# An eight-core two-layer trunk: weight loads held behind the last residual load, the last tile in halves, and norm sums rounded once to bf16

## The chip, the cores and the metric

The kernel runs on all eight cores of one Trainium2 chip, one batch element per core; the cores do not exchange data. Cores 0 to 3 form one die, cores 4 to 7 the other. The metric is the device time of the slowest core, in microseconds (us). The engines are TensorE (PE in the profile), VectorE (DVE), ScalarE (ACT), GpSimd (POOL) and SyncE (SP, which here only issues transfers).

In the fast state every core was granted about 0.99 of the full TensorE clock. In the slow state the cores of one die, or of both, had a visibly lower clock, and the run took up to 3340 us.

## The reference

It is a decoder trunk for batch 8, sequence 4096 and width 1024. Cut to what matters:

```python
for layer in range(2):
    sh1, sc1, g1, sh2, sc2, g2 = ada_modulation(c, ada_w[layer], ada_b[layer])
    h = rmsnorm(x, norm_mix_g[layer]) * (1.0 + sc1) + sh1
    y = mixer_0(h) if layer == 0 else mixer_1(h)     # projections in, mixing, one projection out
    x = x + g1 * y
    h = rmsnorm(x, norm_ffn_g[layer]) * (1.0 + sc2) + sh2
    hid = jnp.square(jax.nn.relu(h @ w_ff1[layer]))  # 1024 -> 4096
    x = x + g2 * (hid @ w_ff2[layer])                # 4096 -> 1024
return rmsnorm(x, final_g)
```

## The kernel before

Each core works through four stages (mixer 0, feed-forward 0, mixer 1, feed-forward 1), each in eight tiles of 512 positions. Between stages the residual stream `xs` lives in HBM: a stage loads it (`load_x`), norms it, and at its end adds to it piece by piece (`residual`). The program is a graph. A list scheduler, with its own model of costs, fixes one static order per engine, by `key`, and semaphore waits are then put where the graph has a dependency.

The norm sums eight squares in float32. It then splits the sum into two bf16 numbers, so that TensorE can sum over partitions with little loss, which takes two products:

```python
def norm_stats(get, Bn, dst, b_dst, key, adds):
    for c in range(8):                    # squares on ScalarE, adds on GpSimd or VectorE into dst (f32)
        # ... cut ...
    act(... activation(out=sqt[:, 0, :], in_=dst, func=AF.Copy) ...)                        # bf16 part
    dve(... tensor_tensor(out=sqt[:, 1, :], in0=dst, in1=sqt[:, 0, :], op=ALU.subtract) ...) # the rest
    pe([(lambda e, i=i: e.matmul(bk(Bn), onesD, sqt[:, i, :], start=i == 0, stop=i == 1), ...)
        for i in range(2)], [Bn], key)
    # ... cut: Ln, Exp
```

The residual add, and the load of a weight:

```python
def residual(ph, ti, c, B, l, grp, key, after=()):
    s = npiece[0] % 8                                             # eight pieces in turn
    dma("sp", ... e.dma_start(out=piece[:, s, :], in_=ap[:, 0, :]) ..., key - 12, ..., after)   # load
    dve(... scalar_tensor_tensor(out=piece[:, s, :], in0=bk(B), ..., in1=piece[:, s, :], ...), key)  # add
    dma("sp", ... e.dma_start(out=xs_d[ph][ti, :, c, :], in_=piece[:, s, :]) ..., key)          # store

def load_weight(k, name, kind, src, key, after=()):
    # ... cut
    dma("pool", lambda e: e.dma_start(out=v, in_=src), [], [b], key, wsem[k], 2 * 1024 * 1024, after)
```

`after` keeps the scheduler from placing an operation before the other has been placed, and nothing more. The waits on the chip come from `pdeps`, which `after` never enters:

```python
# schedule()
for op in self.ops:
    for d in op.after:
        op.npend += 1
        d.succ.append((op, None))      # an order in the list schedule
# emit_orders()
for pi, pd in enumerate(op.pdeps):     # only these become semaphore waits
    ...
```

In a feed-forward, tile 0 runs its second product in blocks, so that it can begin before all weights are there:

```python
w1 = [load_weight(..., base - 40 + i, after[i:i + 1]) for i in range(8)]
w2 = [load_weight(..., base - 30 + i) for i in range(8)]
for ti in range(ntiles):
    # ... cut: 32 groups of 8 products of 128x512 (w1), relu, square
    if ti + 1 < ntiles:
        stage_a(ph, ti + 1, hT, hb, b + TF - 60, b + TF - 45, "dve", [begun])   # load, norm, modulate
    # ... cut: 256 products (w2), then residual adds, or in the last stage the final norm and the stores
```

## Time and profile before

Before the change the kernel took 2825.24 us, the median of three runs (2820.91 to 2830.31).

The opening lines of the page of the kernel before: span, then each engine's busy time, share of the span and instructions.

```profile
span 2822.9 us, 41582 instructions; the slowest of 8 cores (2789.6 to 2822.9 us)
...
PE 2721.0 (96%) x14197; PEld 1267.0 (45%) x14197; DVE 1266.1 (45%) x2171; ACT 1246.0 (44%) x1974; POOL 521.7 (18%) x697
```

TensorE is what bounds the kernel. Inside a stage, time is its number of products; what else there is to win lies at the joints between stages. The cores also differ by 33 us, although all run the same program on data of the same shapes.

I cut the span at landmarks of TensorE: the first value projection of mixer 0, the last output projection of each mixer, the first product with `w_ff2` in each feed-forward, the first value projection of mixer 1, the last main product. For the slowest core (7) and as means over the eight cores of the same execution:

| stage (us) | core 7 | mean |
|---|---|---|
| start | 68.2 | 68.2 |
| mixer 0 | 580.2 | 578.9 |
| joint 0: last projection to first `w_ff2` product | 47.5 | 45.0 |
| feed-forward 0 | 844.6 | 846.0 |
| mixer 1 | 359.9 | 359.5 |
| joint 1 | 69.7 | 57.2 |
| feed-forward 1 | 836.4 | 836.3 |
| tail: last main product to the end | 16.4 | 16.4 |

Three cores (0, 5 and 6) waited nowhere of note at joint 1, and took 46.8 to 46.9 us; the slowest took 69.7.

The list of waits of TensorE on core 7 before, 540 to 760 us and then 1820 to 2000 us. A line names the waiting engine and source line, what it waited for, the total in us, the number of waits and the longest.

```profile
PE ps L713 <- DVE sb_arena L704: 5.6, 2, 3.8
PE ps L665 <- ACT sb_arena L662: 1.3, 1, 1.3
...
PE ps L713 <- DVE sb_arena L704: 17.3, 4, 6.3
```

L704 is the residual add. TensorE's first feed-forward products (L713) wait for a bank of PSUM, which comes free when the add has read it. L665 is the norm product. The add itself waits for its load. This is the view of that one line, 1830 to 1940 us, with what it waited for, us and times:

```profile
  DMA sb_arena<-xs: 36.4, 4
```

What is in the way of those loads are weights. The timeline of GpSimd on core 7 before, at the end of mixer 1; columns are start, length, engine, line, operation, and in brackets the idle time before and its releaser:

```profile
1856.00 0.59 POOL L570 DMA_DIRECT2D sb_arena<-w_ff  x1 [10.83 <-PE ps L1146]
...
1877.41 1.15 POOL L1193 TENSOR_TENSOR sb_arena<-sb_arena 128x512 bf16<-128x512 f32 x1 [5.34 <-DVE sb_arena L1188]
```

Weights of the next stage go out as soon as the buffer that they overwrite is read (L1146 is the value projection), before the last tile's multiplies (L1193).

The tail on core 7 before, from the timeline: last residual add, square, add, the subtract of the split (L663), eight multiplies, stores (the steps between are left out).

```profile
2806.95 0.75 DVE L1057 SCALAR_TENSOR_TENSOR sb_arena<-ps,sb_arena 128x512 f32<-128x512 f32 x1 [4.64 <-PE ps L1032]
...
2810.05 0.69 DVE L663 TENSOR_TENSOR sb_arena<-sb_arena 128x512 bf16<-128x512 f32 x1 [0.83 <-ACT sb_arena L662]
...
2813.08 5.39 DVE L1065 SCALAR_TENSOR_TENSOR sb_arena<-sb_arena 128x512 f32<-128x512 f32 x8 [2.34 <-ACT sb_arena L669]
2813.91 4.97 SPq L1069 DMA_DIRECT2D out<-sb_arena  x8
```

### The profile page before, as it was taken

The page shows a single profiled execution, that of the slowest core. Times are in us where ns is not written, and L with a number is a line of the kernel's source. Part 1 is how long each engine was busy: PE and PEld are TensorE (multiplying, and loading weights), DVE is VectorE, ACT ScalarE, POOL GpSimd, SP SyncE. Part 2 cuts the span into 40 slices and gives each one's busy share as a digit, 9 for nine tenths or more (in the row PEclk, how much of TensorE's full clock was granted, in tenths as well). Part 3 has the DMA queues.
Part 4 walks back from the last instruction along what each step waited for, and adds up shares of the span by engine and source line. Part 5 has one row for each costly group of instructions (what it writes and reads, how often), then busy time and mean ns, then how long its engine had stood idle before and what let it go on. Part 6 is the DMA issues. An engine that isn't in the chain of part 4 may idle for free.

```text
span 2822.9 us, 41582 instructions; the slowest of 8 cores (2789.6 to 2822.9 us)
## 1 busy us (share of the span) xinstructions
PE 2721.0 (96%) x14197; PEld 1267.0 (45%) x14197; DVE 1266.1 (45%) x2171; ACT 1246.0 (44%) x1974; POOL 521.7 (18%) x697
## 2 busy tenths in 40 slices
PE   3999999999999999999999999997999999999997
PEld 1444444444444444444444444443444444444443
DVE  3567777771332232231323777752343243342332
ACT  5788888862333132141224765642343243242330
POOL 5456555440000000000002444230000000000000
PEclk9999999999999999999999999998999999999999
DMA  9743344479423323223354465576021020220110
GB/s 190 146 120 106 105 105 106 116 141 186 140 53 79 81 65 91 68 64 104 78 109 136 137 185 155 168 140 158 31 90 60 31 90 16 75 90 1 60 60 30
DMA packets 111375, 279.96 MB, mean 99 GB/s; under 512 B 12352, under 2 KB 12864, under 8 KB 104384
## 3 DMA queue, kind: packets, MB, share of 16 engines
q1 hardware_dynamic: 92016, 198.65, 22.4%
q0 software_dynamic: 19152, 78.65, 16.7%
q8 instruction: 117, 1.92, 0.3%
q14 instruction: 90, 0.74, 0.1%
HBM read 284.59 MB, written 67.11 MB: 125 GB/s over the span
## 4 chain that ended last, share of the span: by engine, by line
PE 81%; DMA 8%; ACT 4%; issue 3%; DVE 2%; POOL 2%; another core or an unknown queue 0%; SPq 0%; DVEq 0%; ACTq 0%; POOLq 0%
PE ps L713 38%; PE ps L1032 31%; DMA xs<-sb_arena 4%; PE ps L1146 3%; PE ps L1200 3%; PE ps L981 2%; PE ps L954 2%; DMA sb_arena<-xs 2%; DMA sb_arena<-w_in 1%; ACT L408 1%; DMA sb_arena<-x 1%; PE ps L665 1%; PE ps L610 0%; ACT sb_arena L691 0%; PE ps L1183 0%
## 5 line engine op out<-in xcount | busy, mean ns | idle before, releaser
L713 PE MATMUL ps<-sb_arena 128*128 128x512 bf16 x6144 | 1376.7, 381 | 29.4 <-DVE sb_arena L704 22.9
L713 PEld LDWEIGHTS ps<-sb_arena 128*128 128x128 bf16 x6144 | 595.5, 98 | 733.3 <-issue 46.7
L1032 PE MATMUL ps<-sb_arena 128*128 128x512 bf16 x4096 | 890.3, 379 | 0.0
L1021 ACT ACTIVATE sb_arena<-ps 128x512 bf16<-128x512 f32 x512 | 305.0, 597 | 874.3 <-PE ps L713 806.8
L1032 PEld LDWEIGHTS ps<-sb_arena 128*128 128x128 bf16 x4096 | 398.8, 98 | 477.4
L1023 DVE TENSOR_TENSOR sb_arena<-sb_arena 128x512 bf16<-128x512 bf16 x512 | 218.5, 427 | 482.7 <-ACT sb_arena L1021 480.1
L658 ACT ACTIVATE sb_arena<-sb_arena 128x512 f32<-128x512 f32 x280 | 172.9, 625 | 383.3 <-DVE sb_arena L1057 333.5
L704 DVE SCALAR_TENSOR_TENSOR sb_arena<-ps,sb_arena 128x512 f32<-128x512 f32 x192 | 142.9, 746 | 435.6 <-PE ps L1032 312.9
L687 DVE SCALAR_TENSOR_TENSOR sb_arena<-sb_arena 128x512 f32<-128x512 f32 x256 | 195.1, 788 | 42.5 <-ACT sb_arena L669 23.1
L691 ACT ACTIVATE sb_arena<-sb_arena 128x512 bf16<-128x512 f32 x256 | 179.0, 721 | 66.0 <-DVE sb_arena L687 51.0
L408 ACT ACT_TABLE_LOAD x138 | 177.1, 1283 | 39.6 <-PE ps L713 23.5
L629 POOL DMA_DIRECT2D sb_arena<-ada_w x72 | 39.5, 549 | 807.1 <-PE ps L610 785.5
L660 POOL TENSOR_TENSOR sb_arena<-sb_arena 128x512 f32<-128x512 f32 x112 | 149.4, 1334 | 181.2 <-ACT sb_arena L658 171.7
L1057 DVE SCALAR_TENSOR_TENSOR sb_arena<-ps,sb_arena 128x512 f32<-128x512 f32 x64 | 48.0, 751 | 268.1 <-PE ps L1032 267.4
L660 DVE TENSOR_TENSOR sb_arena<-sb_arena 128x512 f32<-128x512 f32 x168 | 116.0, 690 | 83.2 <-ACT sb_arena L658 75.5
L981 PE MATMUL ps<-sb_arena 128*128 128x512 bf16 x512 | 119.8, 379 | 0.0
L1146 PE MATMUL ps<-sb_arena 128*128 128x512 bf16 x512 | 119.5, 379 | 0.0
L1200 PE MATMUL ps<-sb_arena 128*128 128x512 bf16 x512 | 117.8, 379 | 0.3 <-POOL sb_arena L1193 0.2
L1193 POOL TENSOR_TENSOR sb_arena<-sb_arena 128x512 bf16<-128x512 f32 x64 | 75.3, 1193 | 70.1 <-DVE sb_arena L1188 68.6
L1200 PEld LDWEIGHTS ps<-sb_arena 128*128 128x128 bf16 x512 | 50.0, 98 | 61.0 <-issue 1.2
L981 PEld LDWEIGHTS ps<-sb_arena 128*128 128x128 bf16 x512 | 49.5, 98 | 57.7 <-issue 0.2
L1146 PEld LDWEIGHTS ps<-sb_arena 128*128 128x128 bf16 x512 | 49.2, 98 | 55.3
(113 smaller groups left out, 1713.1 us busy)
## 6 DMA issues: line engine op xcount, KB each, us to landing
xs<-sb_arena SPq DMA_DIRECT2D x192, 256.0 KB, 3.7
sb_arena<-xs SPq DMA_DIRECT2D x96, 512.0 KB, 6.2
sb_arena<-xs SPq DMA_DIRECT2D x192, 256.0 KB, 4.1
sb_arena<-w_ff POOLq DMA_DIRECT2D x32, 1024.0 KB, 16.2
sb_arena<-ada_w POOLq DMA_DIRECT2D x72, 256.0 KB, 4.0
sb_arena<-x SPq DMA_DIRECT2D x64, 256.0 KB, 3.6
out<-sb_arena SPq DMA_DIRECT2D x64, 256.0 KB, 3.3
sb_arena<-x SPq DMA_DIRECT2D x24, 512.0 KB, 5.9
```

What stands on the lines that cost most here:

```text
L408: eng.preload_act_table_set(op.table)
L658: act(lambda e, c=c, ap=ap: e.activation(out=tmp[:, c % 2, :], in_=ap, func=AF.Square), [b], [tmpb[c % 2]], key, c_act(512))
L660: G.add(adds, lambda e, c=c: e.tensor_tensor(out=dst, in0=dst, in1=tmp[:, c % 2, :], op=ALU.add), [b_dst, tmpb[c % 2]], [b_dst], key, c_po ...
L687: dve(lambda e, c=c: e.scalar_tensor_tensor(out=tmp[:, c % 2, :], in0=xT[:, c, :], scalar=s1c[:, q, c:c + 1], in1=inv, op0=ALU.mult, op1=A ...
L691: act(lambda e, c=c: e.activation(out=hT[:, c, :], in_=tmp[:, c % 2, :], func=AF.Identity, bias=mod(l, g, c), scale=1.0), [tmpb[c % 2], mo ...
L713: parts = [(lambda e, kc=kc: e.matmul(bk(B), w[:, kc, col0:col0 + 128], hT[:, kc, :], start=kc == 0, stop=kc == 7), [wb, hb[kc]], c_mm(512 ...
L981: pe([(lambda e, kk=kk, c=c, B=B, wv=wv, yc=yc: e.matmul(bk(B), wv[:, kk, (c % 4) * 128:(c % 4) * 128 + 128], yc[:, kk, :], start=kk == 0, ...
L1021: act(lambda e, B=B, q=q: e.activation(out=rt[:, q, :], in_=bk(B), func=AF.Relu), [B], [rtb[q]], k, c_act(512, True))
L1023: dve(lambda e, q=q, fc=fc: e.tensor_tensor(out=hid[:, fc, :], in0=rt[:, q, :], in1=rt[:, q, :], op=ALU.mult), [rtb[q]], [hidb[fc]], k, c_ ...
L1032: return pe([(lambda e, fc=fc, c=c, B=B: e.matmul(bk(B), w2[fc // 4][0][:, fc % 4, c * 128:(c + 1) * 128], hid[:, fc, :], start=fc == 0, s ...
L1146: o = pe([(lambda e, kc=kc, g=g, hh=hh, B=B, hT=hT: e.matmul(bk(B), hT[:, kc, g * 128:(g + 1) * 128], win[2 + hh][0][:, kc, :], start=kc == 0,
L1200: pe([(lambda e, kk=kk, c=c, B=B, wv=wv: e.matmul(bk(B), wv[:, kk, (c % 4) * 128:(c % 4) * 128 + 128], ymix[:, kk, :], start=kk == 0, stop ...
```

## The change

It has three parts. (1) The norm's sum is written as bf16 by the last add, so that one product replaces two and the copy and the subtract go. (2) The last tile of the last stage is computed in halves of 256 positions, so that the norm, the multiplies and the stores of the first half run under the products of the second, and what follows the last product is half as wide. (3) Weight loads are "held" behind the last residual load of the stage before, and in mixer 0 the projections of the tile before the last get earlier keys.

```diff
@@ norm_stats: part 1
-                G.add(adds, lambda e, c=c: e.tensor_tensor(out=dst, in0=dst, in1=tmp[:, c % 2, :], op=ALU.add), ...
-            act(lambda e: e.activation(out=sqt[:, 0, :], in_=dst, func=AF.Copy), ...
-            dve(lambda e: e.tensor_tensor(out=sqt[:, 1, :], in0=dst, in1=sqt[:, 0, :], op=ALU.subtract), ...
-            pe([(lambda e, i=i: e.matmul(bk(Bn), onesD, sqt[:, i, :], ...) for i in range(2)], [Bn], key)
+                to, b_to = (dst, b_dst) if c < 7 else (sqt[:, 0, :], sqb[0])
+                G.add(adds, lambda e, c=c, to=to: e.tensor_tensor(out=to, in0=dst, in1=tmp[:, c % 2, :], op=ALU.add), ...
+            pe([(lambda e: e.matmul(bk(Bn), onesD, sqt[:, 0, :], start=True, stop=True), ...)], [Bn], key)
@@ phase_m0: part 3, layer 0 (ld is the residual's load)
-                    k = b + T0 + (8 + 2 * c if ti + 1 == ntiles else 18 + 4 * c)
+                    k = b + T0 + (18 + 4 * c if ti + 2 < ntiles else 12 + 1.8 * c if ti + 2 == ntiles else 8 + 2 * c)
-                    residual(0, ti, c, B, 0, 2, k, [first])
+                    ld = residual(0, ti, c, B, 0, 2, k, [first])
+            return [()] * 2 + [[ld]] * 14
@@ phase_m1: part 3, layer 1
-            return marks
+            return [[m] for m in marks[:6]] + [[ld]] * 10
@@ phase_ffn
-            w1 = [load_weight(..., base - 40 + i, after[i:i + 1]) for i in range(8)]
-            w2 = [load_weight(..., base - 30 + i) for i in range(8)]
+            w1 = [load_weight(..., base - 40 + i, after[i]) for i in range(8)]
+            w2 = [load_weight(..., base - 30 + i, after[8 + i]) for i in range(8)]
+            def last_tile(ti, b):                                   # part 2
+                for h in range(2):
+                    for c in range(8):
+                        # ... cut: 32 products of 256 columns, residual add, square, add (the 8th square goes
+                        #     to TensorE by itself), for c in (2, 3) a multiply by the gain on GpSimd
+                    # ... cut: norm by two products, Ln, Exp
+                    for c in range(8):
+                        # ... cut: c in (2, 3) multiplied on GpSimd, the six others on VectorE; stores in pairs
+                if final and ti + 1 == ntiles:
+                    last_tile(ti, b)
+                    continue
```

## The prediction

> **What bounds the kernel now.** TensorE is busy 96% of the span (page, first part) and all 760 us from 2000 to 2760 (stretches by engine). 128x512 matmuls start 0.216 us apart (64 in 13.84 us in the chain). The Trainium skill, "TensorE: Matmul & The Clock Gate", section "Wait — 56ns, not 53.3ns?", gives 215.7 ns warm: the trace agrees. Inside a stage only fewer matmuls help; at the joints waits do. On the slowest core (7) these are:
> - start: 33.6 us on adaLN weights, untouched;
> - layer 0 mixer to feed-forward: 5.6 us of TensorE waiting for the residual add;
> - layer 1 mixer to feed-forward: 17.3 us of the same wait (waits list, 1820 to 2000), then clock 0.83 and 0.66 in 1900 to 1940: together about 22 us;
> - end: 16.1 us after the last main matmul (timeline: add 0.75, square 0.63, add 0.69, copy 0.63, subtract 0.69, two matmuls, Ln 0.69, Exp 0.63, eight multiplies 5.39, 4.4 to the end).
> The third is bandwidth: the adds wait 36.4 us for residual loads, whose buffers wait for stores that take over 20 us under weight loads. It falls on cores 1, 3, 4, 7; cores 0, 2, 5, 6, one of each pair, lose at most 1.3 us there and end at 2790 to 2798. The skill's "HBM Reference", "Specifications (TRN2)", says the two cores of a domain share bandwidth; the trace fits, without proving it.
>
> **What the change does.**
> 1. Norm sums: 40 norms lose one matmul, one copy, one subtract. On TensorE 38 x 0.216 = 8 us (estimate from the pitch); the rest is off the path. Expected: -8.
> 2. Last tile in halves: 512 matmuls of 256 columns replace 256 of 512. At 128 columns the trace shows four in 0.39 us, about 55 ns apart with new weights each, so 256 should keep near 108 ns: no cost. After the last matmul remain add 0.48, square 0.42, one exposed matmul 0.55, Ln 0.48, Exp 0.42, six multiplies of 0.41, gaps 0.6, store 4.4: 9.8 us (estimate). Expected: -6.
> 3. Hold, layer 0: the second-last tile's projections move earlier in the program itself, so the last residual loads should precede the burst of weight loads (from 581 us). Expected: -5; the weights are mostly held by their own buffers anyway and should not run late.
> 4. Hold, layer 1: doubtful. "after" enters the list schedule only; no semaphore is waited on. What holds a weight on the chip is its place in GpSimd's queue and its buffer. By my reading the last residual load is placed near 1874 us of this trace, before the last tile's first GpSimd multiply at 1877; then the first weights still go out at 1856 and the wait remains. If they land behind the multiplies (end 1888), about 20 us go on the slow cores. Weighted: -9.
>
> Sum -28: **2796 us**, range 2774 to 2814 (8 in 10). Faster by over 2%: 0.05; within 2%: 0.94; slower by over 2%: 0.01.
>
> **Signs.** Norm: 40 norm products, not 80. Halves: 9 to 11 us from last main matmul to end; the 512 matmuls take 55 to 56 us. Layer 0: no wait for the residual add from 540 to 760, none for feed-forward weights. Layer 1: if TensorE still waits over 8 us for the residual add and the first held weight goes out over 15 us before the last GpSimd multiply, the hold did nothing there.
>
> **What would make it wrong.** Held weights late in tile 0 of a feed-forward; 256-column matmuls slower than 108 ns; the new static order waiting elsewhere; both cores of each pair now stalling together; or the hold working fully, giving 2775.

## The result, and the profile after

The kernel after took 2819.1 us, the median of four runs (2816.86 to 2820.91), against 2826.4 us for the kernel before in the same rounds (four runs, 2820.91 to 2830.31). The ratio is 0.9975 (95% interval 0.9956 to 0.9994). Ratios in this text are the mean time of one kernel's fast runs over that of the other's fast runs of the same rounds, so they are not quite the ratio of the medians that are quoted. On two other chips the same kernel later gave 0.9956 (0.989 to 1.0021) and 0.9958 (0.9936 to 0.9979).

So the change won 7 us where 28 were expected. The time lies outside the predicted range of 2774 to 2814.

The opening lines of the page of the kernel after:

```profile
span 2815.2 us, 41944 instructions; the slowest of 8 cores (2785.6 to 2815.2 us)
...
PE 2711.2 (96%) x14416; PEld 1287.8 (46%) x14416; DVE 1241.1 (44%) x2148; ACT 1209.4 (43%) x1934; POOL 520.3 (18%) x705
```

TensorE is 9.8 us less busy, VectorE 25 and ScalarE 37. The split over the stages shows where the gain went:

| stage (us) | before, core 7 | after, core 2 | before, mean | after, mean | difference of means |
|---|---|---|---|---|---|
| start | 68.2 | 68.3 | 68.2 | 68.8 | +0.6 |
| mixer 0 | 580.2 | 571.3 | 578.9 | 570.9 | -8.0 |
| joint 0 | 47.5 | 39.9 | 45.0 | 39.9 | -5.1 |
| feed-forward 0 | 844.6 | 858.6 | 846.0 | 855.5 | +9.5 |
| mixer 1 | 359.9 | 361.3 | 359.5 | 359.8 | +0.3 |
| joint 1 | 69.7 | 70.4 | 57.2 | 64.6 | +7.4 |
| feed-forward 1 | 836.4 | 834.3 | 836.3 | 834.2 | -2.1 |
| tail | 16.4 | 11.1 | 16.4 | 11.1 | -5.3 |

The 13.1 us won in mixer 0 and joint 0 are followed by 9.5 us lost in feed-forward 0. Joint 1, where the largest gain was hoped for, has none.

The waits of TensorE on core 2 after, in the same two stretches. L663 is the norm product here, L661 the norm's add, L702 the residual add.

```profile
PE ps L663 <- DVE sb_arena L661: 13.9, 1, 13.9
...
PE ps L712 <- DVE sb_arena L702: 19.7, 3, 15.1
```

The first wait has grown: 1.3 us before on core 7, 13.9 after on core 2 (over all cores at most 7.3 us before, and 9.5 to 13.9 after). It is put down to the norm's add, but the add ends a chain that began with a transfer. These are three lines each from the timelines of core 7 before and core 2 after: the run of `w_ff2` products ahead of tile 1's norm product, the first square of that norm, and the norm product.

```profile
695.91 23.47 PE L1032 MATMUL ps<-sb_arena 128*128 128x512 bf16 x108
...
712.09 0.63 ACT L655 ACTIVATE sb_arena<-sb_arena 128x512 f32<-128x512 f32 x1 [18.72 <-DMA sb_arena<-xs]
...
720.71 0.38 PE L665 MATMUL ps<-sb_arena 128*128 128x512 bf16 x1 [1.32 <-ACT sb_arena L662]
```

```profile
679.49 24.34 PE L1091 MATMUL ps<-sb_arena 128*128 128x512 bf16 x112
...
710.49 0.63 ACT L655 ACTIVATE sb_arena<-sb_arena 128x512 f32<-128x512 f32 x1 [31.82 <-DMA sb_arena<-xs]
...
717.73 0.58 PE L663 MATMUL ps<-sb_arena 128*128 128x512 bf16 x1 [13.90 <-DVE sb_arena L661]
```

TensorE begins the `w_ff2` products 16.4 us earlier (679.49 for 695.91). The residual stream of tile 1 lands only 1.6 us earlier (710.49 for 712.09). The norm product stands after 112 of 256 products, where TensorE now arrives at 703.8 us, and nothing later in its static order can go ahead of it. Why the stream doesn't land earlier is seen in the stretches by engine. The columns are stretch, length, busy time of PE, PEld, DVE, ACT and POOL with counts, the granted clock, the busy share of the core's 16 DMA engines, and GB/s. First core 7 before, then core 2 after:

```profile
700.00:710.00 10.00, 10.00 (x48) 4.57 (x47) 0.00 (x0) 0.00 (x0) 0.00 (x0) 1.00 0.98 272
```

```profile
700.00:710.00 10.00, 3.82 (x18) 1.56 (x16) 0.00 (x0) 0.00 (x0) 0.00 (x0) 0.92 0.99 252
```

In both kernels the DMA engines are nearly always full from about 590 to about 710 us (the same view has a DMA share of 1.03 before and 0.99 after in 590 to 600; the lowest stretch is 0.71, before, in 600 to 610), with the feed-forward weights and, behind them, the stream. The second line also shows that the wait costs clock: the grant is 0.92 while TensorE starves. It goes on falling, and is still low when TensorE is back at work. These are the next two stretches of core 2 after:

```profile
710.00:720.00 10.00, 2.27 (x6) 0.87 (x7) 5.27 (x9) 6.50 (x11) 0.00 (x0) 0.50 0.44 156
720.00:730.00 10.00, 10.00 (x44) 4.28 (x42) 5.57 (x8) 5.54 (x8) 0.00 (x0) 0.90 0.00 0
```

So the wait costs somewhat more than its own length: after it, TensorE starts 44 products in 10 us where 48 fit.

The kernel before shows the same trade among its own cores, which the prediction overlooked. Cores 0, 4 and 5 did not wait for the residual add (joint 0 of 39.9 us). They waited 2.8, 7.3 and 6.4 us at this norm product instead, and took 846.0, 852.7 and 852.0 us for feed-forward 0. The other five took 47.1 to 50.0 us at the joint, waited at most 1.3 us at the norm product, and took 842.5 to 844.6 us.

The timeline of GpSimd on core 2 after, at the end of mixer 1:

```profile
1854.95 0.59 POOL L570 DMA_DIRECT2D sb_arena<-w_ff  x1 [10.62 <-PE ps L1208]
...
1876.36 1.15 POOL L1255 TENSOR_TENSOR sb_arena<-sb_arena 128x512 bf16<-128x512 f32 x1 [5.34 <-DVE sb_arena L1250]
```

It is the picture of before, 1 us earlier: no weight is held. The cause is in the static order. Of the ten weights that the change puts behind the last residual load, all stand at the same places of GpSimd's queue as before (679, 680, 681, 683, 690 and 692 to 696, counted from 0). With and without the two `return` lines of the diff the whole of GpSimd's queue is the same, 705 operations. On SyncE's queue 18 places of 639 hold another operation (10 if only the source line is compared), and on each of the three other engines 10 to 13 do. In the scheduler's own model the hold does act: it puts the first of these weights at 1914 us and not at 1894. But GpSimd's queue has nothing else to place there in between, so its order stays as it was, and on the chip GpSimd doesn't wait for the load.

The tail on core 2 after, second half of the last tile:

```profile
2804.52 0.48 DVE L1029 SCALAR_TENSOR_TENSOR sb_arena<-ps,sb_arena 128x256 f32<-128x256 f32 x1 [1.97 <-PE ps L1024]
...
2807.11 3.40 DVE L1059 SCALAR_TENSOR_TENSOR sb_arena<-sb_arena 128x256 f32<-128x256 f32 x6 [2.11 <-ACT sb_arena L1051]
2807.21 1.82 POOL L1056 TENSOR_TENSOR sb_arena<-sb_arena 128x256 f32<-128x256 f32 x2 [14.36 <-ACT sb_arena L1051]
```

The subtract is gone, each step is shorter, and six multiplies take 3.40 us where eight took 5.39. That is 0.57 us each, not the 0.41 that I had estimated. The same six multiplies of the first half ran in two groups, the first four beside GpSimd and the last two while it was idle:

```profile
2781.25 2.61 DVE L1059 SCALAR_TENSOR_TENSOR sb_arena<-sb_arena 128x256 f32<-128x256 f32 x4 [0.92 <-ACT sb_arena L1051]
...
2784.18 0.86 DVE L1059 SCALAR_TENSOR_TENSOR sb_arena<-sb_arena 128x256 f32<-128x256 f32 x2
```

That is 0.65 us each beside GpSimd and 0.43 alone. It fits what the Trainium skill states in "SBUF — State Buffer", section "SBUF: two separate sides": a VectorE operation with two inputs in SBUF and a GpSimd operation that reads SBUF exclude each other on a shared pair of ports. No run here moved the two multiplies off GpSimd, so the lock itself is not shown; only the slower multiplies are.

### The profile page after: what moved, and what is told of

It is laid out like the page before. It is cut to its first block, busy times and chain, and to the rows that moved or that the text cites. A ratio compares the mean times of both kernels' runs of the same rounds, so it can differ in the third digit from the quotient of the medians.

```text
span 2815.2 us, 41944 instructions; the slowest of 8 cores (2785.6 to 2815.2 us)
## 1 busy us (share of the span) xinstructions
PE 2711.2 (96%) x14416; PEld 1287.8 (46%) x14416; DVE 1241.1 (44%) x2148; ACT 1209.4 (43%) x1934; POOL 520.3 (18%) x705
## 4 chain that ended last, share of the span: by engine, by line
PE 86%; DMA 5%; ACT 2%; issue 2%; DVE 1%; POOL 1%; another core or an unknown queue 1%; DVEq 0%; ACTq 0%; SPq 0%; POOLq 0%
PE ps L712 42%; PE ps L1091 28%; PE ps L1208 4%; PE ps L980 3%; PE ps L1262 3%; DMA xs<-sb_arena 2%; PE ps L1024 2%; PE ps L953 2%; DMA sb_arena<-w_in 1%; DMA sb_arena<-xs 1%; DMA sb_arena<-x 1%; ACT L408 1%; PE ps L1245 0%; POOL sb_arena L661 0%
## 5 line engine op out<-in xcount | busy, mean ns | idle before, releaser
L712 PE MATMUL ps<-sb_arena 128*128 128x512 bf16 x6144 | 1374.6, 381 | 25.8 <-DVE sb_arena L702 19.7
L712 PEld LDWEIGHTS ps<-sb_arena 128*128 128x128 bf16 x6144 | 595.0, 98 | 727.4 <-issue 42.2
L1091 PE MATMUL ps<-sb_arena 128*128 128x512 bf16 x3840 | 836.9, 380 | 0.0
L1091 PEld LDWEIGHTS ps<-sb_arena 128*128 128x128 bf16 x3840 | 374.3, 98 | 448.6 <-issue 2.8
L702 DVE SCALAR_TENSOR_TENSOR sb_arena<-ps,sb_arena 128x512 f32<-128x512 f32 x192 | 142.8, 746 | 408.0 <-PE ps L1091 316.8
L661 POOL TENSOR_TENSOR sb_arena<-sb_arena 128x512 f32<-128x512 f32 (+1 forms) x112 | 149.0, 1331 | 181.2 <-ACT sb_arena L658 171.5
L1041 POOL TENSOR_SCALAR sb_arena<-sb_arena 128x256 f32<-128x256 f32 x4 | 4.6, 1144 | 868.5 <-ACT sb_arena L1034 868.5
L661 DVE TENSOR_TENSOR sb_arena<-sb_arena 128x512 f32<-128x512 f32 (+1 forms) x161 | 111.3, 691 | 90.1 <-ACT sb_arena L658 82.6
L1119 DVE SCALAR_TENSOR_TENSOR sb_arena<-ps,sb_arena 128x512 f32<-128x512 f32 x56 | 41.9, 751 | 221.2 <-PE ps L1091 220.6
L1208 PE MATMUL ps<-sb_arena 128*128 128x512 bf16 x512 | 119.6, 379 | 0.0
L980 PE MATMUL ps<-sb_arena 128*128 128x512 bf16 x512 | 118.8, 379 | 0.0
L1262 PE MATMUL ps<-sb_arena 128*128 128x512 bf16 x512 | 118.2, 379 | 0.2 <-POOL sb_arena L1255 0.2
L1255 POOL TENSOR_TENSOR sb_arena<-sb_arena 128x512 bf16<-128x512 f32 x64 | 75.0, 1187 | 68.8 <-DVE sb_arena L1250 67.2
L1262 PEld LDWEIGHTS ps<-sb_arena 128*128 128x128 bf16 x512 | 50.0, 98 | 60.9 <-issue 0.7
L980 PEld LDWEIGHTS ps<-sb_arena 128*128 128x128 bf16 x512 | 49.6, 98 | 57.9 <-issue 0.8
```

Of the source, the lines that this page charges most:

```text
L661: G.add(adds, lambda e, c=c, to=to: e.tensor_tensor(out=to, in0=dst, in1=tmp[:, c % 2, :], op=ALU.add), [b_dst, tmpb[c % 2]], [b_to], key, ...
L712: parts = [(lambda e, kc=kc: e.matmul(bk(B), w[:, kc, col0:col0 + 128], hT[:, kc, :], start=kc == 0, stop=kc == 7), [wb, hb[kc]], c_mm(512 ...
L980: pe([(lambda e, kk=kk, c=c, B=B, wv=wv, yc=yc: e.matmul(bk(B), wv[:, kk, (c % 4) * 128:(c % 4) * 128 + 128], yc[:, kk, :], start=kk == 0, ...
L1091: return pe([(lambda e, fc=fc, c=c, B=B: e.matmul(bk(B), w2[fc // 4][0][:, fc % 4, c * 128:(c + 1) * 128], hid[:, fc, :], start=fc == 0, s ...
L1208: o = pe([(lambda e, kc=kc, g=g, hh=hh, B=B, hT=hT: e.matmul(bk(B), hT[:, kc, g * 128:(g + 1) * 128], win[2 + hh][0][:, kc, :], start=kc == 0,
L1262: pe([(lambda e, kk=kk, c=c, B=B, wv=wv: e.matmul(bk(B), wv[:, kk, (c % 4) * 128:(c % 4) * 128 + 128], ymix[:, kk, :], start=kk == 0, stop ...
```

## The experiments

There were fourteen runs, each with the kernel before on the same chip. All gave the right result but one. The stage means of all:

| run (mean over cores, us) | mixer 0 | joint 0 | feed-forward 0 | the three together | joint 1 | tail |
|---|---|---|---|---|---|---|
| before | 578.9 | 45.0 | 846.0 | 1469.9 | 57.2 | 16.4 |
| after | 570.9 | 39.9 | 855.5 | 1466.3 | 64.6 | 11.1 |
| norm_only (cores 2 and 3 left out) | 571.0 | 41.2 | 851.8 | 1464.0 | 59.4 | 14.7 |
| halves_only | 578.5 | 43.5 | 847.2 | 1469.2 | 61.7 | 10.8 |
| key_only | 577.9 | 40.0 | 857.6 | 1475.5 | 62.3 | 16.3 |
| no_hold_key | 569.5 | 39.9 | 855.2 | 1464.6 | 58.2 | 11.1 |
| after_again | 569.7 | 39.9 | 856.2 | 1465.8 | 66.8 | 11.1 |
| real_hold1 | 570.4 | 39.9 | 856.5 | 1466.8 | 43.4 | 10.8 |
| late_norm | 570.8 | 39.9 | 841.3 | 1452.0 | 66.9 | 11.1 |
| real_hold1_late | 570.9 | 39.9 | 841.1 | 1451.9 | 43.4 | 10.8 |
| half_w2 (wrong result) | 575.7 | 39.9 | 841.4 | 1457.0 | 67.6 | 11.1 |
| best_nokey | 570.6 | 42.0 | 872.2 | 1484.8 | 43.4 | 10.8 |
| no_hold_key2 | 569.8 | 39.9 | 854.3 | 1464.0 | 58.0 | 11.1 |
| after_third | 570.1 | 39.9 | 854.0 | 1464.0 | 63.5 | 11.1 |
| best_plain0 | 571.3 | 40.5 | 841.4 | 1453.2 | 43.4 | 10.8 |
| best_again | 571.5 | 39.9 | 841.3 | 1452.7 | 43.4 | 10.8 |

### The parts one by one

My theory after reading the traces was that the norm and halves terms are real, that the projections placed earlier in mixer 0 remove one wait and make another, and that the hold does nothing. A rival was that the hold, not the earlier keys, costs the time in feed-forward 0. Everything that a run leaves out was put back as it was; with all parts put back, the static order is exactly that of the kernel before.

**norm_only** keeps only part 1:

```diff
-                    k = b + T0 + (18 + 4 * c if ti + 2 < ntiles else 12 + 1.8 * c if ti + 2 == ntiles else 8 + 2 * c)
+                    k = b + T0 + (8 + 2 * c if ti + 1 == ntiles else 18 + 4 * c)
-                if final and ti + 1 == ntiles:
-                    last_tile(ti, b)
-                    continue
```

and no `after` but the one of before.

> The kernel before with the norm sums alone changed (40 norm products fewer). My account: about 8 us less TensorE work, spread over the stages, so ratio to before 0.996 to 0.999; in tile 0 of the first feed-forward TensorE waits at the norm product less than 4 us, as before. Rival (the shortened norm chain is what moved that norm product forward into a wait): the 9 to 14 us wait at the norm product of tile 0, seen after the whole change, is here too, and the time is not below before.

Measured: 0.9992 (0.9952 to 1.0032). Its four fast runs were 2815.97, 2817.01, 2819.07 and 2838.77 us. The last was the profiled one, in which cores 2 and 3 took some 20 us longer over mixer 0 than the others (their clock over the whole run was 0.980 and 0.985), so I leave these two out of its stage means. Mixer 0 fell by 8 us, as in the full change. But feed-forward 0 rose by 6, and TensorE waited 6.5 to 12.5 us at the norm product of tile 1 on seven cores (2.4 on core 5, which first waited 5.8 for the residual add); the expectation of less than 4 us was missed. So that wait doesn't need the earlier keys. The rival is right in part: in the static order the norm product stands behind 96 products here, and also in key_only, where it stands behind 108 in the kernel before. The 12 products are 2.6 us (12 x 0.216). The rest fits what norm_only and key_only also share: TensorE gets to feed-forward 0 earlier.

**halves_only** keeps only part 2 (`last_tile`, with the two-product norm elsewhere).

> The kernel before with the last tile in halves alone. My account: last main matmul to end 10.5 to 11.5 us instead of 16.3, everything earlier as before: 4 to 6 us less, ratio 0.998. Rival (the halves cost on TensorE what they save at the end): the 512 matmuls of 256 columns take over 58 us and the ratio is 1.000.

Measured: 0.9985 (0.997 to 1.0), about -4 us. The tail is 10.8 us. The 512 products of 256 columns take 0.9 us more than the 256 of 512 did (56.2 us busy for 55.3), so the net is about -4.7 us.

**key_only** keeps only the earlier keys in mixer 0 (the `12 + 1.8 * c` of the diff).

> The kernel before with only the second-last tile's projections of layer 0 moved earlier. My account: the wait for the residual add between layer 0's mixer and feed-forward goes (5 to 7 us on the slow cores), the first second product starts 8 to 12 us earlier, and 8 to 13 us of it are given back as a wait at the norm product of tile 0, because both the weights and tile 1's residual stream still have to pass saturated DMA queues; time within 4 us of before. Rival (that wait comes from the norm sums or from held weights): no wait over 5 us at that norm product, and 8 us or more faster.

Measured: 1.0024 (1.0006 to 1.0042), fast runs 2827.94, 2833.36 and 2833.91 us. It is about 7 us slower than the kernel before. Joint 0 has lost its wait (40.0 us), and feed-forward 0 has gained 11.6 us; all cores wait 9.8 to 15.1 us at the norm product. The expectation of within 4 us of before was missed: more was lost than had been won. Part of it is the place of the norm product (96 for 108, 2.6 us), part the clock after the wait: on core 0 it was 0.73 from 720 to 730 us, where TensorE was busy for 9.15 us and started 32 products; 48 fit in 10 us. The two were not split further.

**no_hold_key** is the change without the hold:

```diff
-            return [()] * 2 + [[ld]] * 14
+            return [()] * 16
-            return [[m] for m in marks[:6]] + [[ld]] * 10
+            return [[m] for m in marks] + [()] * 8
```

> The whole change without the hold of weights, the earlier projections kept. My account: the static order on GpSimd is the same with and without the hold, not one weight load changes place, so the time is within 4 us of the whole change's 2819 and TensorE waits as long for the residual add before the second feed-forward (12 to 20 us on most cores). Rival (the hold works, for better or worse): over 8 us away from the whole change, with the waits before either feed-forward different.

Measured: 0.9952 (0.9932 to 0.9971), fast runs 2808.54 to 2816.82 us. Against the kernel before this is 12.6 us less, where the full change had won 7 in its own rounds, so the expectation of within 4 us is not met across the two chips; the intervals of the two ratios overlap, and the pair no_hold_key2 and after_third below compares them on one chip. Every stage of layer 0 is like that of the full change, so the rival falls there: the hold is not what costs time in feed-forward 0.

The third column from the right of the table says why the parts don't add up. From the start of mixer 0 to the start of mixer 1, norm_only wins 5.9 us, key_only loses 5.6, and together in no_hold_key they win 5.3. All of them get TensorE earlier to a point that is set by the DMA engines.

### What binds feed-forward 0, and joint 1

**after_again** is the kernel after, run beside the next three on their chip.

> The whole change once more, on the chip of the next three runs, as their yardstick: ratio to before 0.996 to 0.999, waits at the norm product of tile 0 (9 to 15 us) and for the residual add before the second feed-forward (4 to 20 us by core).

Measured: 0.9956 (0.989 to 1.0021), with only two fast runs of six (2821.26 and 2825.52 us).

**real_hold1** makes the hold real at layer 1: weights 6 to 15 wait on the chip for the landing of the last residual load.

```diff
-        def load_weight(k, name, kind, src, key, after=()):
+        def load_weight(k, name, kind, src, key, after=(), landed=()):
-            dma("pool", lambda e: e.dma_start(out=v, in_=src), [], [b], key, wsem[k], 2 * 1024 * 1024, after)
+            op = dma("pool", lambda e: e.dma_start(out=v, in_=src), [], [b], key, wsem[k], 2 * 1024 * 1024, after)
+            for d in landed:
+                G._dep(op, d, True, 0.0, op.pdeps[0])     # a dependency, so a semaphore wait
```

The theory was that the wait at joint 1 comes from the order of one core's own loads and stores. The rival, from the prediction, was that it comes from two cores sharing a memory's bandwidth; then holding a core's own weights, which moves as many bytes, would leave some pairs waiting.

> The whole change, and ten weights of the second feed-forward wait on the chip, by a semaphore, for the landing of the last residual load. My account (the residual loads are late because the weight loads fill the queues, and the hold as written moves no weight): the wait for the residual add from 1820 to 2000 us falls under 2 us on every core, from last projection to first second product about 47 us on all cores instead of 54 to 72, slowest core 15 to 25 us less than the whole change; TensorE does not wait for weights. Rival (the wait comes from the two cores of a pair sharing their memory, whatever the order of loads): over 8 us of wait remain on half of the cores and under 8 us are gained.

Measured: 0.9857 (0.9815 to 0.99), runs 2792.83 to 2797.03 us. Joint 1 takes 43.4 us on every core, and the residual add's wait for its load is gone from the list. The timeline of GpSimd on core 6, at the end of mixer 1:

```profile
1875.81 1.16 POOL L1259 TENSOR_TENSOR sb_arena<-sb_arena 128x512 bf16<-128x512 f32 x1 [32.02 <-DVE sb_arena L1254]
1876.90 0.59 POOL L570 DMA_DIRECT2D sb_arena<-w_ff  x1
...
1888.60 2.71 POOL L570 DMA_DIRECT2D sb_arena<-w_ff  x5
```

Now the first held weight goes out at 1876.90, behind the first multiply, and the bulk at 1888.60. The waits of TensorE on that core, 1820 to 2000 us:

```profile
PE ps L1266 <- POOL sb_arena L1259: 0.6, 1, 0.6
```

17.3 to 19.7 us of waiting have become 0.6. By core, this run's spans are 2781.9 (core 2) to 2791.1 us (core 6), so the spread fell from 33 us to 9. (43.4 us is less than even the cores without a wait took before, 46.8. Mixer 1 took 362.0 us here for 359.8, so some of that is work moved across the landmark: the edit also changes 45 places of TensorE's order. I did not look further. Over the whole span the mean of the cores fell from 2808.7 us in after_again to 2787.6, so about 21 us are net.) The rival falls as a cause of this wait. The same weights over the same shared memories cost nothing once each core sends them after its own residual loads. The prediction's list of stalled cores (1, 3, 4, 7, one of each pair) also did not survive: in the profiled run after, all eight take more than the 46.8 us of a core without waits.

One thing was not separated. Through the added dependency the scheduler also changes GpSimd's order, in 13 places: the first multiply of the last tile now stands ahead of the first held weight, and all eight multiplies ahead of eight of the ten held weights, where it had been five. In the same trace the last residual load is issued at 1872.36 us, and loads of that line from 1860 to 1880 us land after 2.8 to 5.2 us:

```profile
1872.36 0.32 SPq L702 DMA_DIRECT2D sb_arena<-xs  x1
```

So the load has landed at about the time at which that first multiply ends, and the semaphore had little left to hold back. That weights sent after the residual loads remove the wait is shown. Whether the semaphore does it, or the new places in the queue alone would, is not.

**late_norm** tests the other wait. Tile 1's norm product in feed-forward 0 is placed behind 204 of the 256 products in place of 112. Nothing else in the static order changes but 12 places on VectorE (8 if only the source line is compared).

```diff
-        def norm_stats(get, Bn, dst, b_dst, key, adds):
+        def norm_stats(get, Bn, dst, b_dst, key, adds, behind=()):
-                 c_mm(512))], [Bn], key)
+                 c_mm(512))], [Bn], key, behind)
@@ phase_ffn, layer 0, tile 0
+                                if (h, i, c) == (1, 2, 3):
+                                    late = p
+                    if not final:
+                        stage_a(ph, 1, hT, hb, b + TF - 60, b + TF - 45, "dve", [begun], [late])
```

> The whole change, with the norm product of tile 1 of the first feed-forward moved from behind 112 to behind 204 of the 256 second products of tile 0; no other order changes but eight places on VectorE. My account (TensorE arrives there before the data, which have 90 products' time to spare): the 9 to 15 us wait goes, from first second product to the second mixer's first product about 845 us instead of 855, on all cores alike; 5 to 12 us less than the whole change unless the next joint takes it back. Rival (the DMA queues are behind by that much, so the wait moves to whatever needs a load next): TensorE then waits as long for weights or for tile 1's modulated tile, under 3 us gained at that joint.

Measured: 0.9888 (0.9837 to 0.9939), fast runs 2802.13 to 2806.61 us. Feed-forward 0 fell from 855.5 to 841.3 us. The timeline on core 0:

```profile
679.19 44.19 PE L1091 MATMUL ps<-sb_arena 128*128 128x512 bf16 x200
723.22 0.38 PE L663 MATMUL ps<-sb_arena 128*128 128x512 bf16 x1
```

TensorE starts its products as early as in the kernel after, and comes to the norm product at 723.22 without a wait, since the stream has landed by then. (The line counts 200 products and not 204, because a few records are missing from the trace; 44.19 us are 204 x 0.216.) Here what was won in mixer 0 and joint 0 is kept: the three stages together take 1452.0 us, 17.9 less than before.

**real_hold1_late** has both edits.

> Both together. My account: gains add, every core near 2785, slowest core 2780 to 2795, ratio to before 0.984 to 0.990. Rival: less than the better of the two alone plus 5 us.

Measured: 0.9802 (0.976 to 0.9845), four fast runs of 2779.21 to 2780.25 us. It beats both kernels; whether by over 2% the interval leaves open. The opening of its page:

```profile
span 2778.4 us, 41679 instructions; the slowest of 8 cores (2768.7 to 2778.4 us)
```

### Is it the amount of data, and what is the hold worth

**half_w2** asks whether the stream of tile 1 lands late because the weights are ahead of it in the DMA engines. It loads half of each `w_ff2` weight of layer 0, so 4 MB of 16 MB fewer in that stage, and multiplies by the loaded half twice. Its result is wrong (relative error 0.653).

```diff
+            if name.startswith("w2_0"):
+                dma("pool", lambda e: e.dma_start(out=v[:, 0:2, :], in_=src[:, 0:2, :]), [], [b], key, wsem[k], ...)
+                return v, b
-                        bk(B), w2[fc // 4][0][:, fc % 4, c * 128:(c + 1) * 128], ...
+                        bk(B), w2[fc // 4][0][:, fc % (4 if l else 2), c * 128:(c + 1) * 128], ...
```

> The whole change, but each second weight of the first feed-forward loaded by half only (its other half is not used; the result is wrong on purpose); no order of TensorE, VectorE or ScalarE changes. My account (the wait at the norm product is for the DMA queues to get through 16 weight loads): 4 MB of 16 fewer end the saturated stretch about 20 us earlier, the 9 to 15 us wait falls under 2 us on all cores, and from first second product to the second mixer's first product 841 to 845 us. Rival (the place of the norm product in the order, or its chain of sums, makes the wait by itself): 8 us or more remain.

Measured, in one look: feed-forward 0 takes 841.0 to 842.1 us on every core, with no change of the order on TensorE. The timeline on core 3, and the stretches by engine of the same core:

```profile
682.48 0.63 ACT L659 ACTIVATE sb_arena<-sb_arena 128x512 f32<-128x512 f32 x1 [3.26 <-DMA sb_arena<-xs]
...
704.21 0.38 PE L667 MATMUL ps<-sb_arena 128*128 128x512 bf16 x1
```

```profile
680.00:690.00 10.00, 10.00 (x48) 4.55 (x47) 5.19 (x8) 5.19 (x9) 0.00 (x0) 1.00 0.72 274
690.00:700.00 10.00, 10.00 (x48) 4.55 (x47) 0.00 (x0) 0.00 (x0) 0.00 (x0) 1.00 0.01 2
```

The stream lands 28 us earlier (682.48 for 710.49), the DMA engines are idle from 690 us, and the norm product goes at 704.21 without a wait. So the wait is the queue of bytes in the DMA engines. The Trainium skill says in "DMA: Bandwidth & Descriptors", section "Issuing engines are not separate DMA queues", that transfers run on the same 16 DMA engines and interleave whichever engine starts them. That fits: these weights are started by GpSimd, the stream by SyncE. The run's whole time, 2825.83 us, says little, because two cores ran late elsewhere at a clock of 0.982 and 0.983.

**no_hold_key2** and **after_third** are the change without and with the hold, again, side by side on a third chip.

> The whole change without the hold, on the same chip as the next run: if the hold as written does nothing, within 3 us of it; if its ten changed places on SyncE's queue cost, 4 to 8 us faster than it, and from last projection to first second product of layer 1 shorter by as much on the mean of the cores (58 against 65 to 67 us, as in the profiles so far).

> The whole change as yardstick for the run without the hold: 0.996 to 0.998 of before, and from last projection to first second product of layer 1 a mean of 65 to 67 us over the cores, if the hold's places on SyncE's queue cost; as the run without the hold, if they do not.

Measured: 0.9949 (0.9928 to 0.9969) without, 0.9958 (0.9936 to 0.9979) with. The medians of the fast runs are 2814.2 and 2816.5 us. Means at joint 1 are 58.0 and 63.5 us, but the waits there fall on other cores from run to run. If the hold as written does anything to the time, it is within 2 to 3 us, which these runs don't resolve.

**best_nokey** is real_hold1_late without the earlier keys in mixer 0. I thought that they might be useless.

> Semaphore hold and late norm product together as before, but the second-last tile's projections of layer 0 left where they were. If the earlier projections earn their place once the norm product no longer waits: some residual-add wait before the first feed-forward (0 to 7 us by core) and up to 7 us slower than 2780. If not: within 3 us of 2780.

Measured: 0.9941 (0.9917 to 0.9965), well short of real_hold1_late's 0.9802 and 0.9842, and the expectation missed. Feed-forward 0 takes 872.2 us. One line of the timeline of core 1:

```profile
719.25 40.72 PE L1095 MATMUL ps<-sb_arena 128*128 128x512 bf16 x176 [28.02 <-ACT sb_arena L1084]
```

TensorE waits 28 us in the middle of tile 0. The wait is put down to a relu (L1084), and rightly. These are two lines of ScalarE's timeline on that core:

```profile
717.47 0.63 ACT L657 ACTIVATE sb_arena<-sb_arena 128x512 f32<-128x512 f32 x1 [39.30 <-DMA sb_arena<-xs]
...
718.52 1.07 ACT L1084 ACTIVATE sb_arena<-ps 128x512 bf16<-128x512 f32 x2
```

The last relus of tile 0 stand behind the first squares of tile 1's norm in ScalarE's order, and ScalarE waits 39 us there for the stream of tile 1. By then the weights are in: the last of the 16 was issued at 642.3 us and had landed by 713. So the late stream stops TensorE once more, this time by way of ScalarE. Here the hold at layer 0 does move weight loads: the held weights stand later in GpSimd's queue (places 490 onward, where the order without the hold, in best_plain0 below, has 472 onward), and the first of them goes out at 606.01 us, against 582.88 in best_plain0 on the same core. The order on TensorE changes with them: the first product for the second half of the columns, which needs a further bank of PSUM, comes after 32 of the 256 products, and in best_plain0 after 96. Which of the two changes makes the wait was not separated. But the two lines of code that do nothing with one order cost about 30 us with another: best_nokey and best_plain0 differ in them alone, and feed-forward 0 takes 872.2 and 841.4 us.

**best_plain0** also drops the hold at layer 0, and **best_again** is real_hold1_late, on the same chip.

```diff
-                    k = b + T0 + (18 + 4 * c if ti + 2 < ntiles else 12 + 1.8 * c if ti + 2 == ntiles else 8 + 2 * c)
+                    k = b + T0 + (8 + 2 * c if ti + 1 == ntiles else 18 + 4 * c)
-            return [()] * 2 + [[ld]] * 14
+            return [()] * 16
```

> Semaphore hold at layer 1 and late norm product, but layer 0's joint as in the kernel before (no hold, projections not earlier). If the rearrangement there is worth something: TensorE waits 3 to 8 us for the residual add before the first feed-forward, or for weights, and the time is 4 to 10 us over the run with it. If not: no such wait, first value to first second product near 611 us as with it, and within 3 us of it, near 2780.

> The semaphore hold and the late norm product on the whole change, as yardstick on the same chip: 2777 to 2783 us, all cores within 12 us of each other, no wait for the residual add at either joint.

Measured: 0.9839 (0.9825 to 0.9854) and 0.9842 (0.9825 to 0.9858). They are the same. The yardstick's expectation was missed, though: its fast runs took 2785.70 to 2789.61 us and not 2777 to 2783, and its cores lay 17 us apart. On this chip the kernel before was slower too (2830.65 to 2835.86 us), and mixer 1 took 367.1 us in the mean of the cores where real_hold1_late had 362.6; why was not looked into. Once the norm product of tile 1 stands late and the weights at layer 1 go out behind the residual loads, what the change did to the order of layer 0 is worth nothing that these runs resolve.

## Why the prediction was wrong

It said 2796 us (2774 to 2814); 2819.1 were measured. The class, within 2%, was right. Point by point:

1. **Norm sums, -8 us: right in mechanism; that the size agrees is partly luck.** The trace has 39 full-width norm products and four of half width where there were 80. Mixer 0 fell by 8 us, more than its eight products fewer account for (8 x 0.216 = 1.7 us), and feed-forward 1 by 3.0 in norm_only (836.3 to 833.3), as 14 norms should (14 x 0.216). On core 0, before against norm_only, TensorE's idle time fell by 2.9 us from mixer 0 to the first `w_ff2` product of layer 0, and about 3.7 us of the gain there stay unexplained. Mixer 1 won nothing (359.5 and 359.8 us). But see point 3: alone, norm_only was within the noise of the kernel before.

2. **Halves, -6 us: the mechanism right, the term somewhat too large.** "9.8 us" from the last product to the end was 11.1, mainly because six multiplies of 0.57 us took 3.40 and not the 2.5 of "six multiplies of 0.41". And "no cost" for 512 products of half width was 0.9 us. Net, -4.7 (halves_only; 0.9985, about -4 us in time).

3. **Hold, layer 0, -5 us: this is the step that failed first.** The wait for the residual add did go, on all cores, and joint 0 fell by 5.1 us. The sum then took these 5 us, and the 8 of mixer 0, as kept. They were not: tile 1's norm product stood after 112 products, and the DMA engines were full of weights until about 710 us whatever TensorE did. Arriving 16 us earlier there made a wait of 13.9 us where there had been 1.3. half_w2 (fewer bytes, no wait) and late_norm (the same bytes, a later place, no wait) show this from two sides. The prediction had looked for late weights ("none for feed-forward weights"), not for the stream behind them. Cores 0, 4 and 5 of the kernel before already showed the trade.

4. **Hold, layer 1, -9 us: the reading was right, and the weight put on its opposite was the error.** It said that "after" enters the list schedule only, that the first weights would still go out at 1856, and that the wait would remain. They went out at 1854.95, GpSimd's queue is the same with and without the hold, and the wait is 19.7 us on the slowest core. A sum that gave this item its due would have had 0 here. real_hold1 shows what was there to win: joint 1 from 64.6 to 43.4 us on average.

5. **"Sum -28".** With the measured sizes the differences of means are -13.1 (mixer 0 and joint 0), +9.5 (feed-forward 0), +7.4 (joint 1), -2.1, -5.3 and +0.9 for start and mixer 1; that is -2.7 us as a mean over the cores, against 7.7 on the slowest of the two profiled runs and 7 in the medians. The +7.4 at joint 1 is not shown to be the change's: in the one look at the kernel before, four of the eight cores had no wait or almost none there, and which cores wait changes between runs; the metric takes the slowest core, where joint 1 went from 69.7 to 70.4.

6. **The sharing of bandwidth,** "the trace fits, without proving it" (with the skill's "HBM Reference"): not needed for this wait, as real_hold1 shows.

Open are: the 3.7 us of point 1; whether the port lock is what slows the multiplies; whether the hold as written is worth up to 3 us either way; and whether real_hold1 needs its semaphore or only its new places in GpSimd's queue.

## What to carry to other kernels

Time won ahead of a point that a full DMA queue sets is lost again at that point: before counting a gain, ask what the engine will find when it arrives earlier, and move work that waits for late data behind work that doesn't (14 us here for one changed place). A hold that is only an order in a scheduler holds nothing on the chip unless the queue really moves; compare the static orders, and look in the trace at when the held work really goes out (sending the weights after the residual loads was worth about 21 us here). A wait can also reach an engine through another one's order: the same late stream stopped TensorE at a norm product, and in best_nokey through relus that stood behind it on ScalarE. Parts that push against the same bound don't add up, so test them together as well as alone.

## What the Trainium skill lacked or had wrong

- "TensorE: Matmul & The Clock Gate", section "Seeing it yourself", says to budget 1.95 GHz (13/16 of the clock) for sustained dense matmuls on all cores, on the default power profile. Here all eight cores were dense (TensorE 96% busy), and the granted clock in the fast runs was 0.98 to 0.998, with products 0.216 us apart. Only slow runs showed a die at a lower clock; the lowest, 0.813 to 0.817 on cores 0 to 3 in best_nokey's slow run, is close to those 13/16 (0.8125).
- "GPSIMD Engine Reference", section "4.1 Engine selection", says that GpSimd is roughly at line rate for operations with one input. Here a one-input multiply of 128x256 float32 took 1144 ns on GpSimd on average, and the two-input multiply of the same shape 0.91 us (two in 1.82); times on GpSimd are rough in the trace, but one input was not the cheaper.
- No page that I read gives a number for how late a small transfer lands behind large ones. Here a 256 KB store of the residual stream took 3.7 us as a median from issue to landing in the kernel before, and 18.1 as a median with 36.2 at most from 1830 to 1940 us on core 7, while weights were loading. "DMA: Bandwidth & Descriptors", section "Two DMAs through the same engine are not ordered", tells the issuing engine to wait on the first DMA's semaphore, for a DMA that depends on another's data. It does not say what such an order can save where only time depends on it (joint 1 from 64.6 to 43.4 us in real_hold1, whose queue order changed too).
